# Reordering the start-up loads of an embedding gather: smaller first index load, position table in 256 KB slices, two of them gated

## The chip, the cores and the metric

One core of a Trainium2 chip. The metric is device microseconds of one execution, the median of several.

## The reference

```python
batch, seq_len, vocab_size, d_model = 32, 512, 50000, 512
token_embed = embedding_table[indices]           # indices: int [32, 512]
return (token_embed + position_embed).astype(np.float32)
```

Each of 16,384 table rows (2 KB) is read once, gets the row of its position added and is written out: 33.55 MB in, 33.55 MB out, and 1 MB of position table.

## The kernel before

Partition p holds positions 4p to 4p+3, so a batch row is four gathers (k = 0 to 3) of 128 table rows, 256 KB each, 128 gathers in all. GpSimd issues the gathers, VectorE adds the position slice, SyncE issues loads at the start and stores later, all in order of need. The indices of the first four batch rows come in a small load of their own (`idx0`); the rest (`idx_raw`) are turned by TensorE and used from the 17th gather on.

```python
order = [(b, k) for h in range(2) for b in range(FIRST)
         for k in range(h * half, (h + 1) * half)]        # FIRST = 4, half = 2
order += [(b, k) for b in range(FIRST, B) for k in range(K)]
...
    nc.sync.dma_start(out=idx0[:], in_=idx_first).then_inc(s_first, 16)   # 16 KB
    load_pos(0)                                                           # 512 KB
    nc.sync.wait_ge(s_pos[0], 16)
    load_pos(1)                                                           # 512 KB
    nc.sync.dma_start(out=idx_raw[:], in_=...).then_inc(s_raw, 16)        # 128 KB
...
    nc.gpsimd.wait_ge(s_first, 16)
    for g, (b, k) in enumerate(order):
        if g == FIRST * K:
            nc.gpsimd.wait_ge(s_idx, J)
        ... # slot reuse waits
        ins = nc.gpsimd.indirect_dma_start(out=slots[b % SLOTS][:, k, :], in_=table, ...)
...
    for g, (b, k) in enumerate(order):                    # VectorE
        ...
        nc.vector.tensor_tensor(out=part, in0=part, in1=pos_ps[:, k, :], op=add
            )._wait_ge(s_gather[g % LANES], rounds(g)).then_inc(s_add, 1)
```

Of the kernel before, what the change touches and what calls it, by code (L numbers as in the profile page):

```python
# [8 lines left out]
K = 4  # L9
# [6 lines left out]
@with_exitstack  # L16
def kernel(
    ctx: ExitStack,
    tc: tile.TileContext,
    indices: bass.AP,  # L20
    embedding_table: bass.AP,
    position_embed: bass.AP,
    out: bass.AP,
):






    nc = tc.nc
    f32 = mybir.dt.float32
    i32 = mybir.dt.int32
    add = mybir.AluOpType.add

    B, S = indices.shape
    V, D = embedding_table.shape
    assert S == P * K and B == 32
    assert V < (1 << 24), "an index passes through float32"
    J = P // Q  # L40


    idx_words = indices.bitcast(i32)
    idx_first = idx_words[0:FIRST].rearrange("b (p w) -> p b w", p=P)
    idx_rows = idx_words.rearrange("b (j w) -> (b j) w", j=J)
    out_rows = out.rearrange("b (p k) d -> b p k d", k=K)
    pos_rows = position_embed.rearrange("(p k) d -> p k d", k=K)
    table = embedding_table[:, :]

    def sbuf(name, shape, dtype):  # L50
        return ctx.enter_context(tc.tile_pool(name="p_" + name, bufs=1)).tile(
            shape, dtype, name=name
        )

    def psum(name, shape, dtype):
        pool = tc.tile_pool(name="p_" + name, bufs=1, space=bass.MemoryType.PSUM)
        return ctx.enter_context(pool).tile(shape, dtype, name=name)

    idx0 = sbuf("idx0", [P, FIRST, 2 * K], i32)
    idx_raw = sbuf("idx_raw", [P, Q * K, 2], i32)  # L60
    ones = sbuf("ones", [P, P], f32)
    ident = sbuf("ident", [P, P], f32)
    idx_f = sbuf("idx_f", [P, Q, K], f32)
    idx_t = sbuf("idx_t", [P, K, B], i32)
    pos_sb = sbuf("pos_sb", [P, K, D], f32)
    slots = [sbuf(f"slot{n}", [P, K, D], f32) for n in range(SLOTS)]
    turned = psum("turned", [Q, K, B, J], f32)
    pos_ps = psum("pos_ps", [P, K, D], f32)



    half = K // 2
    order = [(b, k) for h in range(2) for b in range(FIRST)
             for k in range(h * half, (h + 1) * half)]
    order += [(b, k) for b in range(FIRST, B) for k in range(K)]
    stores = []
    for g, (b, k) in enumerate(order):
        if (b == 0 and k < half) or b == B - 1:
            stores.append((g + 1, b, k, 1))
        elif k % half == half - 1:  # L80
            stores.append((g + 1, b, k + 1 - half, half))

    sem = tc.alloc_semaphore
    s_first, s_raw = sem("s_first"), sem("s_raw")
    s_pos = [sem(f"s_pos{h}") for h in range(2)]
    s_gather = [sem(f"s_gather{n}") for n in range(LANES)]

    s_out = {b: sem(f"s_out{b}") for b in range(B - SLOTS)}
    s_rest = sem("s_rest")
    s_ident, s_cast, s_turn, s_idx, s_ps, s_add = (  # L90
        sem(n) for n in ("s_ident", "s_cast", "s_turn", "s_idx", "s_ps", "s_add")
    )

    def rounds(g):
        return 16 * (g // LANES + 1)

    def load_pos(h):
        at = slice(h * half, (h + 1) * half)
        nc.sync.dma_start(out=pos_sb[:, at, :], in_=pos_rows[:, at, :]).then_inc(
            s_pos[h], 16  # L100
        )

    with tc.tile_critical(no_gpsimd_drain=True):  # L103

        nc.sync.dma_start(out=idx0[:], in_=idx_first).then_inc(s_first, 16)
        load_pos(0)
        nc.sync.wait_ge(s_pos[0], 16)
        load_pos(1)
        nc.sync.dma_start(
            out=idx_raw[:], in_=idx_rows.rearrange("r (s w) -> r s w", w=2)  # L110
        ).then_inc(s_raw, 16)


        nc.gpsimd.memset(ones[:], 1.0).then_inc(s_ident, 1)  # L114
        nc.gpsimd.affine_select(  # L115
            out=ident[:], in_=ones[:], pattern=[[-1, P]],
            compare_op=mybir.AluOpType.is_equal, fill=0.0, base=0,
            channel_multiplier=1,
        )._wait_ge(s_ident, 1).then_inc(s_ident, 1)
        nc.gpsimd.wait_ge(s_first, 16)  # L120
        for g, (b, k) in enumerate(order):
            if g == FIRST * K:
                nc.gpsimd.wait_ge(s_idx, J)
            if b >= SLOTS and k == 0:
                done = sum(1 for x in stores if x[1] == b - SLOTS)
                nc.gpsimd.wait_ge(s_out[b - SLOTS], 16 * done)  # L126
            if b < FIRST:
                where = idx0[:, b, 2 * k : 2 * k + 1]
            else:
                where = idx_t[:, k, b : b + 1]  # L130
            ins = nc.gpsimd.indirect_dma_start(  # L131
                out=slots[b % SLOTS][:, k, :],
                out_offset=None,
                in_=table,
                in_offset=bass.IndirectOffsetOnAxis(ap=where, axis=0),
            ).then_inc(s_gather[g % LANES], 16)
            if g >= LANES:
                ins._wait_ge(s_gather[g % LANES], rounds(g - LANES))
        nc.gpsimd.drain()  # L139


        nc.tensor.wait_ge(s_ident, 2)
        for k in range(K):
            ins = nc.tensor.transpose(  # L144
                turned[:, k].rearrange("p b j -> p (b j)"), idx_f[:, :, k], ident[:]
            )
            ins.then_inc(s_turn, 1)
            if k == 0:
                ins._wait_ge(s_cast, 1)


        for g, (b, k) in enumerate(order):
            if g == 7:
                nc.vector.tensor_copy(  # L154
                    out=idx_f[:].rearrange("r p k -> r (p k)"), in_=idx_raw[:, :, 0]
                )._wait_ge(s_raw, 16).then_inc(s_cast, 1)
            if g == 9:
                nc.vector.wait_ge(s_turn, K)
                for j in range(J):
                    nc.vector.tensor_copy(  # L160
                        out=idx_t[j * Q : (j + 1) * Q, :, :], in_=turned[:, :, :, j]
                    ).then_inc(s_idx, 1)
            if b == 0:
                nc.vector.wait_ge(s_ps, k + 1)
            part = slots[b % SLOTS][:, k, :]
            nc.vector.tensor_tensor(  # L166
                out=part, in0=part, in1=pos_ps[:, k, :], op=add
            )._wait_ge(s_gather[g % LANES], rounds(g)).then_inc(s_add, 1)


        for k in range(K):
            nc.scalar.copy(out=pos_ps[:, k, :], in_=pos_sb[:, k, :])._wait_ge(  # L172
                s_pos[k // half], 16
            ).then_inc(s_ps, 1)


        rest = 0
        for adds, b, at, n in stores:
            done = s_out.get(b, s_rest)
            rest += done is s_rest  # L180
            nc.sync.dma_start(
                out=out_rows[b][:, at : at + n, :],
                in_=slots[b % SLOTS][:, at : at + n, :],
            )._wait_ge(s_add, adds).then_inc(done, 16)
        nc.sync.wait_ge(s_rest, 16 * rest)
# [30 lines left out]
```

## Time and profile before

| | kernel before |
|---|---|
| time, median | 177.46 us (3 runs, 177.31 to 177.65) |
| span of the profile | 175.5 us |
| first gather issued / last gather issued | 3.31 / 162.31 us |
| last add starts | 169.96 us |
| DMA share and rate, 60 to 160 us | 1.03, 419 GB/s |

How to read it: GpSimd issues a gather every 1.25 us without a pause, and the DMA engines have no idle time from about 24 us on (share 1.02 to 1.03 in the windows from 24 to 168 us; it adds up packet times and so passes 1). Two windows summarize the start (after stretch and length: busy time of PE, PEld, DVE, ACT, POOL; then the TensorE clock, the DMA share, GB/s):

```profile
4.00:12.00 8.00, 0.00 (x0) 0.00 (x0) 1.38 (x2) 1.79 (x4) 6.12 (x7) 1.00 0.82 266
12.00:24.00 12.00, 1.04 (x4) 0.44 (x4) 7.20 (x14) 0.42 (x1) 9.00 (x10) 1.00 0.96 336
```

### The profile page before, as it was taken

Reading aid. Unit: us, or ns where it says so; the run is one execution under the profiler, and the core shown is the slowest. Engines: PE = TensorE matmul, PEld = TensorE weight load, DVE = VectorE, ACT = ScalarE, POOL = GpSimd, SP = SyncE. Lnnn points to the kernel's source line nnn. Section 1 sums busy time; section 2 is a strip of 40 time slices with the busy share of each in tenths; the row PEclk is TensorE's granted clock in tenths of the full one; section 3 lists DMA queues with packets and bytes.
Section 4 is the critical chain, followed back from the end, with each engine's and each line's share of the span. In section 5 each row is a group of like instructions: output and inputs, shape, how many; then the busy total and the mean of one; then the engine's idle time right before and its main releaser. Section 6 shows DMA issues by size and latency. Waiting matters only on the chain.

```text
span 175.5 us, 423 instructions
## 1 busy us (share of the span) xinstructions
PE 1.0 (1%) x4; PEld 0.4 (0%) x4; DVE 89.1 (51%) x133; ACT 3.5 (2%) x5; POOL 121.9 (69%) x134
## 2 busy tenths in 40 slices
PE   0000100000000000000000000000000000000000
PEld 0000000000000000000000000000000000000000
DVE  0136645555465556465545554565455645554550
ACT  2220000000000000000000000000000000000000
POOL 4777777777777777777777777777777777777200
DMA  4799999999999999999999999999999999999993
GB/s 120 234 316 309 349 383 402 390 410 410 416 412 418 416 419 419 418 418 418 416 421 418 420 418 420 418 418 419 418 416 417 420 418 418 418 419 418 418 413 130
DMA packets 20851, 68.34 MB, mean 389 GB/s; under 512 B 3696, under 2 KB 3824, under 8 KB 20848
## 3 DMA queue, kind: packets, MB, share of 16 engines
q1 hardware_dynamic: 10608, 34.76, 49.0%
q0 software_dynamic: 10240, 33.56, 49.0%
q14 instruction: 3, 0.02, 0.0%
HBM read 34.75 MB, written 33.55 MB: 389 GB/s over the span
## 4 chain that ended last, share of the span: by engine, by line
POOL 66%; issue 24%; DMA 5%; POOLq 1%; DVE 0%; SPq 0%
POOL slot L131 66%; DMA slot<-in_embedding_table_dram,idx_t 4%; DMA idx<-in_indices_dram 1%; POOLq L139 1%; DVE slot L166 0%; POOLq L126 0%; SPq L211 0%; SPq L103 0%
## 5 line engine op out<-in xcount | busy, mean ns | idle before, releaser
L131 POOL DMA_INDIRECT slot<-in_embedding_table_dram,idx_t x112 | 105.9, 946 | 34.1 <-issue 34.1
L166 DVE TENSOR_TENSOR slot<-slot,pos_ps 128x512 f32<-128x512 f32 x128 | 87.9, 688 | 81.5 <-DMA slot<-in_embedding_table_dram,idx_t 63.6
L131 POOL DMA_INDIRECT slot<-in_embedding_table_dram,idx x16 | 15.3, 958 | 6.3 <-issue 4.6
L172 ACT COPY pos_ps<-pos_sb 128x512 f32<-128x512 f32 x4 | 2.2, 586 | 8.0 <-DMA pos_sb<-in_position_embed_dram 8.0
L172 ACT ACT_TABLE_LOAD x1 | 1.3, 1283 | 1.0 <-SPq L103 1.0
L160 DVE CAST idx_t<-turned 32x128 int32<-32x128 f32 x4 | 1.1, 279 | 0.1
L144 PE MATMUL turned<-ident,idx_f 128*32 128x128 f32 x4 | 1.0, 416 | 17.2 <-DVE idx_f L154 17.2
L114 POOL MEMSET ones<- 128x128 f32 x1 | 0.2, 204 | 0.5 <-SPq L103 0.5
L144 PEld LDWEIGHTS turned<-ident,idx_f 128*32 128x32 f32 x4 | 0.4, 133 | 17.3 <-DVE idx_f L154 17.2
L115 POOL TENSOR_SCALAR_AFFINE_SELECT ident<-ones 128x128 f32<-128x128 f32 x1 | 0.3, 287 | 0.1
L200 POOL MEMSET const-float32-0.0<- 128x1 f32 x1 | 0.1, 98 | 0.3 <-issue 0.3
L154 DVE CAST idx_f<-idx_raw 128x128 f32<-128x128 int32 x1 | 0.2, 220 | 0.0
L200 POOL MEMSET const-uint8-127<- 128x1 uint8 x1 | 0.1, 115 | 0.0
L200 POOL MEMSET const-bfloat16-1.0<- 128x1 bf16 x1 | 0.1, 109 | 0.0
L200 POOL MEMSET const-float32-1.0<- 128x1 f32 x1 | 0.1, 101 | 0.0
## 6 DMA issues: line engine op xcount, KB each, us to landing
out_dram<-slot SPq DMA_DIRECT2D x61, 512.0 KB, 6.6
slot<-in_embedding_table_dram,idx_t POOLq DMA_INDIRECT x112, 7.4
out_dram<-slot SPq DMA_DIRECT2D x6, 256.0 KB, 3.9
pos_sb<-in_position_embed_dram SPq DMA_DIRECT2D x2, 512.0 KB, 4.9
slot<-in_embedding_table_dram,idx POOLq DMA_INDIRECT x16, 6.3
idx_raw<-in_indices_dram SPq DMA_DIRECT2D x1, 128.0 KB, 6.2
idx<-in_indices_dram SPq DMA_DIRECT2D x1, 16.0 KB, 2.0
```

Source lines behind the costliest of these rows:

```text
L114: nc.gpsimd.memset(ones[:], 1.0).then_inc(s_ident, 1)
L115: nc.gpsimd.affine_select(out=ident[:], in_=ones[:], pattern=[[-1, P]], compare_op=mybir.AluOpType.is_equal, fill=0.0, base=0, channel_mul ...
L131: ins = nc.gpsimd.indirect_dma_start(out=slots[b % SLOTS][:, k, :], out_offset=None, in_=table, in_offset=bass.IndirectOffsetOnAxis(ap=whe ...
L139: nc.gpsimd.drain()
L144: ins = nc.tensor.transpose(turned[:, k].rearrange("p b j -> p (b j)"), idx_f[:, :, k], ident[:])
L154: nc.vector.tensor_copy(out=idx_f[:].rearrange("r p k -> r (p k)"), in_=idx_raw[:, :, 0])._wait_ge(s_raw, 16).then_inc(s_cast, 1)
L160: nc.vector.tensor_copy(out=idx_t[j * Q : (j + 1) * Q, :, :], in_=turned[:, :, :, j]).then_inc(s_idx, 1)
L166: nc.vector.tensor_tensor(out=part, in0=part, in1=pos_ps[:, k, :], op=add)._wait_ge(s_gather[g % LANES], rounds(g)).then_inc(s_add, 1)
L172: nc.scalar.copy(out=pos_ps[:, k, :], in_=pos_sb[:, k, :])._wait_ge(s_pos[k // half], 16).then_inc(s_ps, 1)
L200: nc = _bacc.Bacc("TRN2", target_bir_lowering=False, num_devices=1)
```

## The change

Its intent: bring the first gather forward by loading only the first batch row's indices ahead of it, fill the DMA engines' idle time before it, and keep the later half of the position table out of the way of the first gathers. The first store of the second batch row is split in two as well.

```diff
-        if (b == 0 and k < half) or b == B - 1:
+        if (b <= 1 and k < half) or b == B - 1:
             stores.append((g + 1, b, k, 1))
...
-        nc.sync.dma_start(out=idx0[:], in_=idx_first).then_inc(s_first, 16)
-        load_pos(0)
-        nc.sync.wait_ge(s_pos[0], 16)
-        load_pos(1)
+        nc.sync.dma_start(out=idx0[:, 0, :], in_=idx_first[:, 0, :]).then_inc(
+            s_first, 16
+        )
+        load_pos(nc.sync, 0)
+        nc.sync.dma_start(out=idx0[:, 1:, :], in_=idx_first[:, 1:, :]).then_inc(
+            s_next, 16
+        )
+        load_pos(nc.sync, 1)
         nc.sync.dma_start(
             out=idx_raw[:], in_=idx_rows.rearrange("r (s w) -> r s w", w=2)
         ).then_inc(s_raw, 16)
+        nc.sync.wait_ge(s_pos[half - 1], 16)
+        load_pos(nc.sync, half)
+        nc.sync.wait_ge(s_gather[0], 16)
+        load_pos(nc.sync, half + 1)
...
         for g, (b, k) in enumerate(order):
+            if g == half:
+                nc.gpsimd.wait_ge(s_next, 16)
...
-                s_pos[k // half], 16
+                s_pos[k], 16
```

`load_pos(engine, k)` now loads one 256 KB slice k.

More of the change, by code (lines that the diff above doesn't have):

```diff
@@ L83 @@
     sem = tc.alloc_semaphore
-    s_first, s_raw = sem("s_first"), sem("s_raw")
-    s_pos = [sem(f"s_pos{h}") for h in range(2)]
+    s_first, s_next, s_raw = sem("s_first"), sem("s_next"), sem("s_raw")
+    s_pos = [sem(f"s_pos{k}") for k in range(K)]
     s_gather = [sem(f"s_gather{n}") for n in range(LANES)]
@@ L95, in rounds, with load_pos @@
         return 16 * (g // LANES + 1)
-    def load_pos(h):
-        at = slice(h * half, (h + 1) * half)
-        nc.sync.dma_start(out=pos_sb[:, at, :], in_=pos_rows[:, at, :]).then_inc(
-            s_pos[h], 16
+    def load_pos(engine, k):
+        engine.dma_start(out=pos_sb[:, k, :], in_=pos_rows[:, k, :]).then_inc(
+            s_pos[k], 16
         )
     with tc.tile_critical(no_gpsimd_drain=True):
-        nc.sync.dma_start(out=idx0[:], in_=idx_first).then_inc(s_first, 16)
-        load_pos(0)
-        nc.sync.wait_ge(s_pos[0], 16)
-        load_pos(1)
+        nc.sync.dma_start(out=idx0[:, 0, :], in_=idx_first[:, 0, :]).then_inc(
[6 more added lines that the diff above has]
+        load_pos(nc.sync, 1)
         nc.sync.dma_start(
@@ L172 @@
             nc.scalar.copy(out=pos_ps[:, k, :], in_=pos_sb[:, k, :])._wait_ge(
-                s_pos[k // half], 16
+                s_pos[k], 16
             ).then_inc(s_ps, 1)
```

## The prediction

> **What bounds the kernel now.** I read the page's DMA rows first, then the chain that ended last, then the start in order of time, then the landing times of the gathers by stage.
>
> The first question is which resource has no slack left. The windows by stage (after the stretch and its length: busy us of PE, PEld, DVE, ACT and POOL; the last two columns are the DMA share and GB/s):
>
> ```profile
> 0.00:2.00 2.00, 0.00 (x0) 0.00 (x0) 0.00 (x0) 1.03 (x1) 0.69 (x6) 1.00 0.00 0
> 2.00:4.00 2.00, 0.00 (x0) 0.00 (x0) 0.00 (x0) 0.26 (x1) 0.69 (x1) 1.00 0.79 221
> 4.00:6.00 2.00, 0.00 (x0) 0.00 (x0) 0.00 (x0) 0.97 (x2) 1.40 (x2) 1.00 0.48 147
> 6.00:8.00 2.00, 0.00 (x0) 0.00 (x0) 0.69 (x1) 0.13 (x1) 1.69 (x2) 1.00 0.90 287
> 8.00:10.00 2.00, 0.00 (x0) 0.00 (x0) 0.00 (x0) 0.00 (x0) 1.39 (x3) 1.00 0.94 313
> ...
> 60.00:160.00 100.00, 0.00 (x0) 0.00 (x0) 54.79 (x81) 0.00 (x0) 75.61 (x81) 1.00 1.03 419
> 164.00:168.00 4.00, 0.00 (x0) 0.00 (x0) 2.29 (x4) 0.00 (x0) 0.00 (x0) 1.00 1.03 421
> ```
>
> The DMA share is 1.03 for 100 us, at 419 GB/s. While GpSimd still feeds it and after GpSimd has issued its last gather (164 to 168), the rate is the same, so about 420 GB/s is what the 16 engines can do with this mix, and bytes that are not moved early are moved at the end. The holes are at the start: 0.48 in 4 to 6, 0.90 and 0.94 after it.
>
> The chain names another engine:
>
> ```profile
> POOL 66%; issue 24%; DMA 5%; POOLq 1%; DVE 0%; SPq 0%
> L131 POOL DMA_INDIRECT slot<-in_embedding_table_dram,idx_t x112 | 105.9, 946 | 34.1 <-issue 34.1
> ```
>
> GpSimd spends 0.946 us on a gather and 0.30 us between two, and idles for nothing else. The starts run from 3.31 to 162.31 us, so 127 steps take 159.0 us, 1.252 us each. One step asks for 256 KB in and 256 KB out: 524,288 B / 1.252 us = 419 GB/s. So the two limits coincide: GpSimd offers almost exactly what the DMA engines can carry. A backlog that exists after the start therefore hardly drains. That is seen in the time from issue to landing of a gather, first for those issued from 3 to 9 us, then from 100 to 164 us:
>
> ```profile
> DMA to landing us min/median/max: 3.5/6.1/6.3
> DMA to landing us min/median/max: 7.0/7.5/7.8
> ```
>
> The first gather took 3.5 us, the late ones 7.5: some 4 us of every gather is queue. The end is the last issue at 162.31, plus 7.63 (the chain's last DMA piece), plus the add's 0.69, plus the last store, to 175.5. A shorter queue would show in that 7.63.
>
> The start in order of time:
>
> ```profile
> 1.02 0.43 SPq L105 DMA_DIRECT2D idx<-in_indices_dram  x1
> 1.52 3.83 SPq L99 DMA_DIRECT2D pos_sb<-in_position_embed_dram  x2
> 3.31 1.14 POOL L131 DMA_INDIRECT slot<-in_embedding_table_dram,idx  x1 [1.72 <-DMA idx<-in_indices_dram]
> 4.75 0.95 POOL L131 DMA_INDIRECT slot<-in_embedding_table_dram,idx  x1 [0.30 <-issue]
> 5.39 0.43 SPq L109 DMA_DIRECT2D idx_raw<-in_indices_dram  x1
> 6.79 0.69 DVE L166 TENSOR_TENSOR slot<-slot,pos_ps 128x512 f32<-128x512 f32 x1 [6.79 <-DMA slot<-in_embedding_table_dram,idx]
> 10.85 0.69 DVE L166 TENSOR_TENSOR slot<-slot,pos_ps 128x512 f32<-128x512 f32 x1 [3.37 <-DMA slot<-in_embedding_table_dram,idx]
> ```
>
> The reader is to see three things. The first gather starts 0.28 us after the index load's landing (1.02 + 2.01 = 3.03 in the chain). The index words for all of idx_raw are issued only at 5.39, after the wait for the first position half. The second gather, issued at 4.75, is added only at 10.85, 6.1 us on: the second position half (512 KB, issued near 5.0, landing 6.3 us later) is on the engines together with it.
>
> [...] two queues with 49.0% of the engines each. So a load on the SP ring can delay a gather, which is what the change works on. [...] the trace stays at 419 to 421, so I use 420. [...]
>
> **The change part by part.**
>
> 1. *First index load, 16 KB to 4 KB.* It is the only thing ahead of the first gather. Of the 512 pieces of 32 B (32 per engine) 128 stay (8 per engine). In the trace's packet records the 512 start between about 2.1 and 2.6 us and land between 2.63 and 3.03. A quarter of them should land about 2.7: all gathers 0.3 us earlier (estimate, 0.2 to 0.4). The second index load is behind one position slice on the ring. SP issues take 0.33 to 0.49 us, so it is issued near 1.9 and lands near 4.3 (estimate: 2.4 us, as for the first load with 256 KB ahead). GpSimd wants it for the third gather, near 5.7. Slack over 1 us, so the new wait costs nothing; the wait that exists before the 17th gather shows no longer step than the others.
>
> 2. *Filling the hole.* Before, only the first position half (512 KB) is moved by the time the first gather's data flow, at about 5.0 us by the packet records. After, slices 0 and 1 and idx_raw are issued without a wait, near 1.5 to 3.1, so 2 x 256 + 128 = 640 KB lie before it. The 128 KB moved out of the saturated time are worth 131,072 B / 420 GB/s = 0.31 us. The hole itself also ends 0.3 us earlier (part 1). These two gains add, since both are idle time of the engines removed.
>
> 3. *Smaller pieces.* A slice is 2 KB per partition, not 4 KB. The packet records show 84 ns for a 2 KB packet and 159 ns for a 4 KB one: 9 ns more per 4 KB. Slices 2 and 3 are 16 packets of 2 KB per engine, 16 x 84 - 8 x 159 = 72 ns more; the split store of the second batch row another 72 ns. Cost 0.14 us.
>
> 4. *Order in the crowded time.* Slice 2 follows slice 1, slice 3 follows the first gather. So 512 KB no longer arrive at once next to gathers 0 and 1. Gather 1 should land 1 to 2 us earlier, and its store and the stores of the second batch row, now split, start earlier. The DMA share between 6 and 16 us has about 0.9 us of idle (from packet records in 1 us slices: 0.80 to 1.00). Earlier stores fill perhaps a third: 0.3 us (the softest term, 0 to 0.6). The loads deferred still take their own bytes; nothing is removed.
>
> Later consumers don't bind: slices 2 and 3 are first used by add 9, which started at 19.47; GpSimd wanted the turned indices at 23.51 and they were there about 21.3.
>
> Sum: -0.3 (part 1) -0.31 (part 2) +0.14 (part 3) -0.3 (part 4) = -0.77 us. I take 0.7 off 177.46: 176.8 us.
>
> **The rivals.** *GpSimd's cadence alone sets the end.* The chain speaks for it: 127 steps without a DMA wait. Then only part 1 counts: -0.3 us, 177.15. Against it speaks the queue of 4 us in each gather, which doesn't drain.
>
> *The whole queue goes.* If the backlog were born of the 512 KB burst alone, gathers would land in 3.5 to 4 us to the end and the time would fall by up to 3.5 us, to 174. Against it: the bytes remain, the gathers' own 4 KB packets average 200 to 230 ns in the first 22 us (159 ns later), by a few slow ones of 300 to 1,200 ns, and the change doesn't touch these. So the queue will build again.
>
> *A new wait takes the place.* The second index load late behind slice 0 stalls GpSimd at the third gather, or slice 3, which waits for the first gather on the ring that also carries stores, holds up the first store. A stall of GpSimd shifts everything after it; a store delay of about 0.33 us of issue is hidden by the add's 0.69. It would make 177.5 to 178.5. The slack in part 1 speaks against it.
>
> **Range and chances.** The terms of which I am sure add to some -0.3, the hopeful ones to -1.3; the three runs lie within 0.34 us. Where slow packets fall may move the end by 0.3. So 175.8 to 177.6 for 8 in 10. Two per cent is 3.55 us. Only the second rival reaches it: 3%. Slower by 2% needs several microseconds of new stalls: 1%. Within 2%: 96%.
>
> **What would show it.** Right: first gather near 3.0 and not 3.31; the DMA share in 4 to 6 us above 0.48; the add of gather 1 before 10; the last gather's issue to landing below 7.6; GpSimd's steps still 1.25 us with no idle at the third gather. Wrong: a first gather that did not move (part 1), a share in 4 to 6 as before (part 2), a landing time at the end of 7.6 with an earlier start (the start's gain is then only the shift), or DMA waits of GpSimd on the indices.

The marked cuts are statements that no trace or run of this case shows, with what was argued from them. No term of the sum is among them: -0.30 - 0.31 + 0.14 - 0.30 = -0.77 us, of which 0.7 was taken off 177.46. The 420 GB/s is the trace's own rate (419 to 422). Two figures are estimates: the 2.4 us of the second index load (in the changed kernel it landed 2.6 us after its issue at 1.93), and the 0.3 us by which slow packets may move the end, which no run shows.

## The result, and the profile after

**176.41 us** (4 runs, 176.13 to 176.63) against 177.48 us for the kernel before (4 runs): 1.07 us less. Ratios are computed as the mean time of one kernel's fast runs over that of the other's of the same rounds, so they are not quite the ratio of these medians: 0.9939, 95% interval 0.992 to 0.9958. Within 2%, but clear of noise.

The start in order of time, from the changed kernel's timeline (start, length, engine, line, what; in brackets the idle time before it and what ended it; other lines are left out):

```profile
1.02 0.38 SPq L105 DMA_DIRECT2D idx<-in_indices_dram  x1
1.93 0.43 SPq L109 DMA_DIRECT2D idx<-in_indices_dram  x1
2.89 1.14 POOL L141 DMA_INDIRECT slot<-in_embedding_table_dram,idx  x1 [1.31 <-DMA idx<-in_indices_dram]
2.93 0.43 SPq L113 DMA_DIRECT2D idx_raw<-in_indices_dram  x1
5.59 0.95 POOL L141 DMA_INDIRECT slot<-in_embedding_table_dram,idx  x1 [0.30 <-issue]
5.79 1.29 SPq L98 DMA_DIRECT2D pos_sb<-in_position_embed_dram  x2
6.76 0.69 DVE L176 TENSOR_TENSOR slot<-slot,pos_ps 128x512 f32<-128x512 f32 x1 [6.76 <-DMA slot<-in_embedding_table_dram,idx]
7.98 0.69 DVE L176 TENSOR_TENSOR slot<-slot,pos_ps 128x512 f32<-128x512 f32 x1 [0.54 <-DMA slot<-in_embedding_table_dram,idx]
11.64 0.69 DVE L176 TENSOR_TENSOR slot<-slot,pos_ps 128x512 f32<-128x512 f32 x1 [2.97 <-DMA slot<-in_embedding_table_dram,idx]
```

The first gather starts at 2.89 us instead of 3.31. The third (5.59) shows the ordinary 0.30 us step: the new wait costs nothing. The second add comes at 7.98 instead of 10.85. But the first add is where it was (6.76, was 6.79), although its gather was issued 0.42 us earlier, and the third is little earlier (11.64, was 12.25).

The windows of the same profile:

```profile
2.00:4.00 2.00, 0.00 (x0) 0.00 (x0) 0.00 (x0) 0.26 (x1) 1.11 (x1) 1.00 0.66 167
4.00:6.00 2.00, 0.00 (x0) 0.00 (x0) 0.00 (x0) 0.79 (x2) 1.39 (x3) 1.00 0.89 290
6.00:8.00 2.00, 0.00 (x0) 0.00 (x0) 0.71 (x2) 0.38 (x1) 1.48 (x2) 1.00 0.82 246
8.00:10.00 2.00, 0.00 (x0) 0.00 (x0) 0.67 (x1) 0.00 (x0) 1.61 (x2) 1.00 0.74 154
4.00:12.00 8.00, 0.00 (x0) 0.00 (x0) 1.74 (x3) 1.77 (x3) 5.87 (x8) 1.00 0.83 236
12.00:24.00 12.00, 1.04 (x4) 0.44 (x4) 7.19 (x15) 0.59 (x1) 9.26 (x10) 1.00 1.03 386
```

The hole in 4 to 6 us is filled (share 0.89, was 0.48), and another has opened in 6 to 10 (0.82 and 0.74, were 0.90 and 0.94). Over 4 to 12 the share is 0.83 and was 0.82: **the hole moved.** Two stretches beside it belong to the picture. From 2 to 4 us the share fell (0.66, was 0.79), so part of the filling is the same loads moved later. From 12 to 24 us more was carried (386 GB/s, was 336); over 0 to 24 us it is 286 GB/s and was 275, some 0.26 MB more, but a second trace of the kernel before, shown later, has 282.

The end, from the chain and the timeline of both profiles, the kernel before first:

```profile
162.31 7.63 DMA slot<-in_embedding_table_dram,idx_t
169.96 0.69 DVE L166 TENSOR_TENSOR slot<-slot,pos_ps 128x512 f32<-128x512 f32 x1 [0.41 <-DMA slot<-in_embedding_table_dram,idx_t]
...
161.86 7.32 DMA slot<-in_embedding_table_dram,idx_t
169.20 0.69 DVE L176 TENSOR_TENSOR slot<-slot,pos_ps 128x512 f32<-128x512 f32 x1 [0.43 <-DMA slot<-in_embedding_table_dram,idx_t]
```

The two profiles differ by 175.49 - 174.42 = 1.07 us, which splits like this:

| piece of the span | before | after | difference |
|---|---|---|---|
| until the first gather is issued | 3.31 | 2.89 | -0.42 |
| 127 steps of GpSimd | 159.00 | 158.97 | -0.03 |
| last gather, issue to landing | 7.63 | 7.32 | -0.31 |
| landing to SyncE passing its last wait | 3.68 | 3.66 | -0.01 |
| closing part, to the end of the span | 1.87 | 1.58 | -0.30 |

(The moment of SyncE's last wait, 173.62 and 172.84 us, is from the trace's instruction records.) The first line is a direct effect of an edit. Whether the last landing and the closing part are effects or scatter is what the experiments had to tell.

### The profile page after: what moved, and what is told of

The parts are those of the page before. It is cut to its first block, busy times and chain, and to the rows that moved or that the text cites. A ratio compares the mean times of both kernels' runs of the same rounds, so it can differ in the third digit from the quotient of the medians.

```text
span 174.4 us, 427 instructions
## 1 busy us (share of the span) xinstructions
PE 1.0 (1%) x4; PEld 0.4 (0%) x4; DVE 89.0 (51%) x133; ACT 3.6 (2%) x5; POOL 121.9 (70%) x134
## 4 chain that ended last, share of the span: by engine, by line
POOL 65%; issue 22%; DMA 8%; DVE 1%; POOLq 1%; SPq 0%
POOL slot L141 65%; DMA slot<-in_embedding_table_dram,idx_t 4%; DMA slot<-in_embedding_table_dram,idx 3%; DMA idx<-in_indices_dram 1%; DVE idx_t L170 1%; POOLq L149 1%; DVE slot L176 0%; POOLq L136 0%; SPq L221 0%; POOLq L133 0%; SPq L102 0%
```

## The experiments

Two theories. **Queue**: the DMA engines are the bound; each microsecond of engine time saved at the start is saved at the end. **Cadence**: GpSimd's steps are the bound, so only the start of the first gather counts.

Twelve runs were made, and a trouble came with them: eleven fell on two chips on which the timings could not resolve tenths.

### The changed kernel again, and the chips with a long closing part

> The changed kernel again, as the measure for this batch. Two theories. Queue: the DMA engines are the bound, so idle time of theirs at the start and every byte they move count at the end. Cadence: GpSimd's 128 steps of 1.25 us are the bound and only the start of the first gather counts. Both: 1.0 us under the kernel before (0.8 to 1.2).

Measured: 183.51 us against 183.29 for the kernel before on the same chip, ratio 1.001 (0.9997 to 1.0023), where both theories expected 1.0 us less. Both kernels are some 6 us slower than on the first chip, and the gain is gone. The page's DMA rows (40 slices of the span, here 4.56 us each) show where the 6 us are:

```profile
DMA  3899999999999999999999999999999999999900
GB/s 107 236 344 336 367 377 387 401 407 412 413 412 417 420 417 418 418 419 419 419 415 420 413 420 418 420 417 418 421 419 420 418 418 411 416 413 421 357 0 0
```

The last two slices are empty: for 9 us nothing moves. In the instruction records SyncE passes its last wait at 173.57 us, about as in the profiles above, but the span ends at 182.24. The closing part takes 8.67 us instead of 1.6 to 1.9: four of SyncE's ten closing instructions take 0.7 or 1.4 us each, while none took over 0.03 us on the first chip. The trace also holds only 421 landing records, where the changed kernel's on the first chip held 3,248. All eleven traces of these two chips hold 401 to 462. Whether the missing records and the long closing part have one cause was not shown: landings are only part of the records (the same traces hold 701 to 776 semaphore updates in all), and no run turns the recording off.

What follows: on these chips the span hardly follows the work, and neither a gain nor a loss of some tenths in it can be trusted. Below, each run's *last add* start is given beside its time. It lies ahead of the closing part and is read from the timeline. It is one look each, and looks at one kernel differ by up to 1.1 us. All looks, in us (the kernels are described in the sections that follow):

| kernel (chips) | first gather | last add | last gather, issue to add | closing part |
|---|---|---|---|---|
| before (first chip; chip 9) | 3.31; 3.20 | 169.96; 170.06 | 7.65; 7.39 | 1.87; 1.87 |
| changed (first chip; chip 5) | 2.89; 2.90 | 169.20; 169.84 | 7.34; 7.60 | 1.58; 8.67 |
| the cut alone (5; 5; 0) | 2.89; 2.88; 3.06 | 169.53; 169.61; 169.44 | 7.67; 7.45; 7.31 | 8.60; 8.39; 9.04 |
| all but the cut (5; 5; 0) | 3.20; 3.33; 3.27 | 170.18; 170.97; 169.86 | 8.02; 8.48; 7.53 | 8.71; 8.11; 9.29 |
| 512 KB less (5; 5; 0) | 2.92; 2.88; 2.89 | 169.05; 169.62; 169.05 | 7.15; 7.79; 7.19 | 9.54; 8.93; 9.71 |
| no gates (5) | 2.89 | 171.09 | 9.01 | 7.60 |

The kernel before has no trace on chips 5 and 0, so a comparison with it goes across chips; the others compare on the same chips. The scatter is not one of reading the last gather alone: averaged over a run's last 32 gathers, the time from issue to add still differs between runs of one kernel by as much (7.52 to 8.48 us without the cut).

### The kernel before, for its trace

> The kernel before itself, for its trace on the chip where the experiments ran: on that chip the closing part after the last wait takes 7.6 to 9.5 us and the spans differ by less than the ends of the work do. If the ends of the work are comparable between chips, SyncE passes its last wait near 173.6 us, as in the profile of the kernel before (the changed kernel: 172.84 there, 173.57 here), and the closing part is 8.4 us or so, the span near 182.0 as in its timed runs.

Measured: 177.41 us beside 178.09 for the same kernel as baseline, one run each. This run fell on another chip than the other experiments, with SyncE's last wait at 173.83 us and a closing part of 1.87 us, as in the first profile. Its last add starts at 170.06 us (169.96 in the first profile). The 0.7 us between two runs of one kernel is a warning. One of its waits was new (engine and line, what it waited for, us in total, times, longest):

```profile
POOL slot L131 <- DVE idx_t L160: 0.8, 1, 0.8
```

GpSimd stood 0.8 us ahead of its 17th gather for the turned indices, 0.5 us more than the 0.3 us of an ordinary step. So the slack that I saw there is not always there: it depends on when the ninth add (19.47 us in the first profile), after which VectorE turns to the indices, gets its gather. Its last gather was issued at 162.67 us (162.31 in the first profile), though its first started 0.11 us earlier: one of the two looks at the kernel before contains a stall.

### The cut of the first index load alone

```diff
 # on the kernel before
-        nc.sync.dma_start(out=idx0[:], in_=idx_first).then_inc(s_first, 16)
+        nc.sync.dma_start(out=idx0[:, 0, :], in_=idx_first[:, 0, :]).then_inc(s_first, 16)
         load_pos(0)
+        nc.sync.dma_start(out=idx0[:, 1:, :], in_=idx_first[:, 1:, :]).then_inc(s_next, 16)
...
+            if g == half:
+                nc.gpsimd.wait_ge(s_next, 16)
```

> Only the index load of the first four batch rows is cut in two (4 KB first, 12 KB after the first position half); position halves, idx_raw and stores as in the kernel before. The first gather should start at 2.9 us instead of 3.31. Cadence: the end moves by as much, -0.4 us, and nothing else is needed. Queue: also about -0.4 us, as the idle stretch before the first gather ends earlier. Neither is told apart by it, but it measures the first term of the sum (I had -0.3).

> The cut of the first index load alone, again, because in the first batch every kernel took 8.6 to 9.5 us from the end of its work to the end of the span (1.6 to 1.9 us in the profiles taken at the prediction), which hides tenths. Read here is also the moment at which SyncE passes its last wait, before that closing part. Both theories: last wait 0.4 us earlier than before's 173.62 us, time -0.4 us. If GpSimd's start is given back in the gathers' landing time (7.65 us from the last issue to the last add in the first batch, as in the kernel before), less.

> The cut of the first index load alone, hoped for on a chip without the long closing part (the kernel before ran its last look on one: span 175.7 us). Both theories: -0.4 us against before, last wait near 173.2 us. On the other chip it was -0.2% and -0.15% (0.3 us).

Measured: 182.93, 182.98 and 183.19 us; ratios 0.9988 (0.9973 to 1.0002), 0.9985 (0.9972 to 0.9998) and 0.9981 (0.9967 to 0.9995), or 0.3 us less each time. The first interval reaches past 1, and the spans on these chips decide little: the changed kernel, which has the same cut, was 0.2 us slower than the kernel before on chip 5. The third batch fell on another of the long-closing chips. The last adds:

```profile
169.53 0.69 DVE L173 TENSOR_TENSOR slot<-slot,pos_ps 128x512 f32<-128x512 f32 x1 [0.59 <-issue]
169.61 0.69 DVE L173 TENSOR_TENSOR slot<-slot,pos_ps 128x512 f32<-128x512 f32 x1 [0.64 <-DMA slot<-in_embedding_table_dram,idx_t]
169.44 0.69 DVE L173 TENSOR_TENSOR slot<-slot,pos_ps 128x512 f32<-128x512 f32 x1 [0.44 <-DMA slot<-in_embedding_table_dram,idx_t]
```

Their mean is 169.53; the changed kernel's two (169.20 and 169.84) have 169.52, so near only by luck, and the kernel before 170.01 (169.96 and 170.06). **This edit alone has all of the gain in the last add that can be seen.**

### All of the change but that cut

```diff
 # on the changed kernel
-        nc.sync.dma_start(out=idx0[:, 0, :], in_=idx_first[:, 0, :]).then_inc(s_first, 16)
+        nc.sync.dma_start(out=idx0[:], in_=idx_first).then_inc(s_first, 16)
         load_pos(nc.sync, 0)
-        nc.sync.dma_start(out=idx0[:, 1:, :], in_=idx_first[:, 1:, :]).then_inc(s_next, 16)
...
-            if g == half:
-                nc.gpsimd.wait_ge(s_next, 16)
```

> The change without the cut of the first index load: one 16 KB load, first gather again at 3.31 us; 256 KB position slices, idx_raw ahead of the waits, gates and split stores stay. Queue: -0.5 to -0.65 us against the kernel before, DMA share in 4 to 6 us near 0.85. Cadence: nothing, 0.0 within 0.15, as GpSimd starts no earlier.

> The change without the cut of the first index load, again. Queue: -0.35 to -0.65 us against the kernel before. Cadence: 0.0 within 0.15. In the first batch it was 0.4 us slower, with the last gather landing 8.0 us after its issue; if that repeats, filling the hole with slices and idx_raw gains nothing and the start of GpSimd is all of the gain.

> All of the change but the cut of the first index load. Queue: -0.35 to -0.65 us against before (the changed kernel's -1.07 less the shift of 0.42). Cadence: 0.0 within 0.15. On the chip with the long closing part it was +0.4 us with the last gathers landing 8.0 and 8.5 us after issue; if the rest truly adds nothing, this is 0.0 or above here too, and the changed kernel's gain over 0.42 us is scatter.

Measured: 183.70, 183.70 and 183.96 us; ratios 1.0022, 1.0021 and 1.0022, each with an interval just above 1. The last adds:

```profile
170.18 0.69 DVE L169 TENSOR_TENSOR slot<-slot,pos_ps 128x512 f32<-128x512 f32 x1 [0.74 <-issue]
170.97 0.69 DVE L169 TENSOR_TENSOR slot<-slot,pos_ps 128x512 f32<-128x512 f32 x1 [0.59 <-issue]
169.86 0.69 DVE L169 TENSOR_TENSOR slot<-slot,pos_ps 128x512 f32<-128x512 f32 x1 [0.27 <-issue]
```

Their mean is 170.34. That is 0.3 us later than the kernel before, with a larger scatter; and each of the three ends later than each of the cut alone, on the same chips. Windows of the first of them:

```profile
4.00:6.00 2.00, 0.00 (x0) 0.00 (x0) 0.00 (x0) 1.18 (x2) 1.39 (x3) 1.00 0.83 246
6.00:8.00 2.00, 0.00 (x0) 0.00 (x0) 0.69 (x1) 0.00 (x0) 1.70 (x2) 1.00 0.74 163
```

The first hole is filled here too (0.83), the next one opened too (0.74), and the end did not come sooner. The 0.35 us or more that Queue asked for are not there. The +0.2% in time I don't read as a loss, no more than the cut's 0.3 us as a gain: both were measured on the chips where the closing part takes 7.6 to 9.7 us.

### 512 KB less to load

```diff
 # on the changed kernel; half of the result is wrong on purpose
-        nc.sync.wait_ge(s_pos[half - 1], 16)
-        load_pos(nc.sync, half)
-        nc.sync.wait_ge(s_gather[0], 16)
-        load_pos(nc.sync, half + 1)
...
-            nc.scalar.copy(out=pos_ps[:, k, :], in_=pos_sb[:, k, :])._wait_ge(
-                s_pos[k], 16
+            nc.scalar.copy(out=pos_ps[:, k, :], in_=pos_sb[:, k % half, :])._wait_ge(
+                s_pos[k % half], 16
```

> The changed kernel without the loads of position slices 2 and 3 (their adds read slices 0 and 1 again, so half of the result is wrong on purpose). 512 KB less to move, GpSimd untouched. Queue: 524,288 B / 420 GB/s = 1.25 us less than the changed kernel (0.8 to 1.4), and the last gathers land in 6.4 us or less instead of 7.3. Cadence: no change within 0.2 us.

> The changed kernel with 512 KB less to load (wrong result on purpose), again. Queue, fully kept: 1.25 us under the changed kernel, some -2.3 us against before. Cadence: like the changed kernel, -1.0. The first batch's traces showed a middle: last gathers landing 0.4 us sooner and the last wait 0.9 us earlier than the changed kernel there; that middle (a removed byte counts about half) would be -1.4 to -1.9 us.

> The changed kernel with 512 KB less to load (wrong result on purpose). Queue, fully kept: -2.3 us against before (-1.07 and -1.25). Cadence: -1.0 as the changed kernel. A byte removed early counting half, as the ends of the work on the other chip suggest: -1.4 to -1.9 us.

Measured: 183.50, 183.57 and 183.62 us, ratios 1.001, 1.0015 and 1.0004. Last adds: 169.05, 169.62 and 169.05 us, mean 169.24: 0.28 us before the changed kernel's 169.52, where Queue expects 1.25. Queue also expected the last gathers to land in 6.4 us or less; the last add came 7.15, 7.79 and 7.19 us after its gather's issue. With a scatter of 0.6 us in both kernels 0.28 is not told from nothing, but 1.25 is far from it. So most of the removed transfer bought nothing. The windows of the third run say why:

```profile
4.00:12.00 8.00, 0.00 (x0) 0.00 (x0) 2.57 (x4) 2.21 (x4) 5.86 (x8) 1.00 0.81 257
12.00:24.00 12.00, 1.04 (x4) 0.44 (x4) 6.48 (x14) 0.00 (x0) 9.26 (x10) 1.00 0.96 335
60.00:160.00 100.00, 0.00 (x0) 0.00 (x0) 54.97 (x80) 0.00 (x0) 75.63 (x81) 1.00 1.03 419
```

With fewer bytes to move the engines simply idle more up to 24 us: 0.96 in 12 to 24, where the changed kernel had 1.03 and 1.00 in its two profiles. By 24 us the three runs had moved 6.24 to 6.41 MB and the changed kernel 6.79 and 6.85: what is missing is the size of the two slices (0.52 MB), so nothing else had moved up into their place. Stores can't fill that time, since a store needs an add and an add needs its landed gather. From 60 us on everything is as before. The queue that exists later is therefore not made of these two loads.

### No gates

```diff
 # on the changed kernel
-        nc.sync.wait_ge(s_pos[half - 1], 16)
         load_pos(nc.sync, half)
-        nc.sync.wait_ge(s_gather[0], 16)
         load_pos(nc.sync, half + 1)
```

> The changed kernel without its two gates: all four position slices are issued as soon as SyncE can, after the index loads, so that they are on the engines before and beside the first gather. Queue: idle time before 6 us shrinks further, -0.2 us against the changed kernel. Rival, order: 512 KB in front of the first two gathers delay their landing by about 1 us and with it the first stores, so +0.2 us against the changed kernel or nothing. GpSimd's steps stay the same in both.

Measured: 183.51 us, ratio 1.0009 (0.9997 to 1.0021), on a long-closing chip. The last add and the windows:

```profile
171.09 0.69 DVE L174 TENSOR_TENSOR slot<-slot,pos_ps 128x512 f32<-128x512 f32 x1 [0.42 <-issue]
...
6.00:8.00 2.00, 0.00 (x0) 0.00 (x0) 0.00 (x0) 0.59 (x1) 1.48 (x2) 1.00 0.94 326
8.00:10.00 2.00, 0.00 (x0) 0.00 (x0) 0.72 (x2) 1.18 (x2) 1.60 (x2) 1.00 0.96 353
4.00:12.00 8.00, 0.00 (x0) 0.00 (x0) 2.40 (x4) 2.36 (x4) 5.86 (x8) 1.00 0.89 298
```

Without the gates the second hole is gone (0.94 and 0.96 in 6 to 10 us), so it was the gated slices that were missing there. This kernel moves the most of all between 4 and 12 us (0.89, 298 GB/s), so by Queue it should end first. It ends last: 171.09, and its last gather, issued at 162.08, was added 9.0 us later. Its first add starts at 8.73 us, 2 us later than in the changed kernel, as the rival (order) expected. One look, so I take only the sign: a fuller start did not bring the end forward. The span, 182.34, does not even show the late end, because the closing part was 7.60 us instead of 8.67.

## Why the prediction was right or wrong

The number was right: 176.41 us lies in 175.8 to 177.6, and the gain of 1.07 stands against the 0.7 foretold. That it came so near is in good part luck: of the four terms of the sum one held, and a part of the gain came from a place that the prediction did not look at.

- **Part 1, the first index load: right, somewhat too small.** "All gathers 0.3 us earlier": 0.42 in the two profiles of the result. Over all looks, the first gather starts at 2.91 us with the cut (nine looks) and at 3.26 without it (five): 0.35 us. The 4 KB load landed after 1.59 us, the 16 KB one after 2.01. The new wait at the third gather cost nothing (the step before it is 0.30 us), as said. This part alone gave the last add of the changed kernel.
- **Part 2, filling the hole: right about the hole, wrong about its worth.** The share in 4 to 6 rose from 0.48 to 0.89. The step that failed is "These two gains add, since both are idle time of the engines removed", with its premise that "bytes that are not moved early are moved at the end". The share over 4 to 12 us stayed at 0.82 and 0.83: the idle time went to 6 to 10 us, where the gated slices were missing (without the gates the share there is 0.94 and 0.96). Nor were 640 KB through ahead of the first gather's data: by the packet records 482 KB were (561 in the second look; 528 before). Without the cut they were (647 to 654 KB), and still the last add came at 170.34 us, not before 170.01.
- **Part 3, smaller pieces:** 0.14 us could not be resolved. (A slip of reading beside it: one window of the kernel before, 160 to 164 us, has 422 GB/s, where the prediction says 419 to 421. It changes nothing.)
- **Part 4, the crowded time: wrong.** Gather 1 was indeed added before 10 us, at 7.98. "Earlier stores fill perhaps a third" of the idle time did not happen from 6 to 10 us, where the share fell; that it rose from 12 to 24 did not show at the end.
- **The first rival, GpSimd's cadence, was nearer to the truth.** It gave 177.15 us with a gain of 0.3. The cut alone ends 0.48 us earlier in the last add, with the scatter and across the chips as said. I had set it aside because the gathers' 4 us of queue "doesn't drain". It doesn't, but 512 KB less of loads hardly shortened it (last gather, issue to add: 7.15, 7.79 and 7.19 us, against 7.34 and 7.60), so that queue is no proof that bytes at the start count.
- **The shorter closing part (-0.30) goes with the length of SyncE's program.** In SyncE's instruction records there is a pause of 0.4 us. In both traces of the kernel before (86 records of SyncE) it stands in front of the fourth instruction after the last wait, and the closing part is 1.87 us in both. With 87 records (the cut alone) it stands in front of the third (0.42 us in one trace, 1.0 in the two others), with 88 (512 KB less) of the second, with 89 (all but the cut) of the first; with 90 (the changed kernel and no gates) it is gone from the closing part, and the one trace of the changed kernel without the long closing has 1.58 us. So the four instructions that the edit adds seem to push the pause ahead into the last wait, where it would cost nothing; this is inferred from its places, the wait itself doesn't show it. The place goes with the number of instructions, not with the order of the loads. What the pause is, the records don't say.
- **The rest.** The interval of the ratio puts the gain between 0.75 and 1.42 us; the cut's 0.42 and the closing part's 0.30 make 0.72. Some 0.35 us remain, about the shorter last landing (-0.31). No experiment shows an edit that makes it, and landings of one kernel scatter by more; but the changed kernel has only one profile and four times on a chip with a short closing part, so that it is scatter isn't shown either.

What sets those 7.3 us from issue to landing stays open. In the traces with full records a gather's 16 engines land apart. The kernel before on chip 9 averages, over its last 32 gathers, 6.28 us for the 14th engine, 6.44 for the 15th and 7.46 for the last, as if one late engine held each gather up; in its first profile they are 6.92, 7.21 and 7.56, without such a gap. Slow gather packets (over 250 ns, where 159 is usual) come mostly before 24 us: 106 of 826 there, 4 of 5,135 from 60 to 160, in the first profile. One could think that engines hit by them early stay late for the whole run. Their number does not bear it out: the runs with 512 KB less have the most (110 to 113) and two of the three land soonest, the run without gates has 75 and lands last. No run removed those packets.

## What to carry to other kernels

When an engine issues at a fixed pace from first to last, look first at what stands ahead of its first issue: here this was the only part of the loads' reordering whose gain could be seen at the end (0.35 us at the start, 0.48 at the last add, within the scatter). A DMA share near 1.0 doesn't prove that every byte counts (here it was 1.03 from 60 to 160 us, and 512 KB less moved the last add by 0.28 us, within the scatter of 0.6): take bytes away and see whether the end moves. And compare where the work ends, not only the span: on two chips here the closing part took 7.6 to 9.7 us, and even on the others 0.30 us of the gain lay in them.
